# TensorE in program order through the sparse attention of a two-block model

## The chip, the cores and the metric

The kernel runs on one core of a Trainium2 chip. The metric is the device time of an execution in microseconds; each time is the median of several runs. All times inside the core count from the start of the profiled span.

## What is computed

Two blocks with two layers each work on 512 tokens of width 1024. The change is in the first block, in its sparse attention, which runs once a layer, so twice. Cut to what matters here:

```
q_rope = partial_rope(rmsnorm(heads(nq, 8)))          # 8 heads of 64, 2 key/value heads
o_cmp = softmax(q_nope @ kc.T * scale, cmp_mask) @ vc  # compressed keys
o_slc = selected_attn(q_rope, k_sl, v_sl, sel)         # top 16 of 8 blocks: all of them
o_win = window_attn(q_rope, k_wn, v_wn)                # window 512: all of the past
o_nsa = g[0] * o_cmp + g[1] * o_slc + g[2] * o_win
y_nsa = o_nsa * silu(nz)
h = h + concat([y_hg, y_nsa]) @ w_out
gate = sigmoid(rmsnorm(h) @ w_pg);  h = h + gate * (p @ w_pp)
```

With 8 blocks of 64 tokens the top 16 are all blocks, so the selected and the window branch are both causal attention over 512 tokens, with keys and values of their own.

## The kernel before

All products of a dense layer are split in a high and a low part of 32-bit floats: a dense product of 128 output columns is 24 matmuls of 512 columns (`acc_fm`, three for each of 8 tiles of the input), in two halves of 12 (`lin_steps`). The weights come in pieces of 512 KB through four buffers, and are split into `whi` (ScalarE) and `wlo` (VectorE, for `nz`, `hgo` and `hz` GpSimd) in two buffers each.

`nsa_pairs` does the two full branches. Heads are taken as four pairs `j`; a pair's two heads lie in the upper and the lower 64 partitions. For each pair the 512 queries are taken in four tiles of 128, from the last (t = 3) to the first, and a tile sees 128 (t + 1) keys. A unit is one tile with one branch (t = 3 and 2) or with both (t = 1 and 0), so a pair has six units with 512, 512, 384, 384, 2 x 256 and 2 x 128 columns for each head, and a layer has 24.

A unit has two parts. `probs` makes the scores of both heads with three products each and adds the causal mask by a product with the identity (L1317, L1319), takes the row maxima on VectorE (L1324, L1326), the exponentials with their sums on ScalarE (L1331), the reciprocal sums times the gate on VectorE (L1335 to L1339), and scales the probabilities, head 0 on VectorE (L1341), head 1 on ScalarE (L1342). `values` transposes the probabilities on TensorE (L1356), copies the transposes out of PSUM, head 0 on VectorE (L1362), head 1 on ScalarE (L1360), and multiplies with the values into one bank for the whole pair (L1369). A pair's last unit adds the compressed branch (L1372, L1373), multiplies with the gate (L1375) and splits. `values` runs two units behind `probs` (`DEEP`).

Between the units, `pump` takes a step of the generator `first_fill`: half a dense product (`nz`, `hgo`, `hz`, four blocks each, then the first part of `ple`), and behind it, as long as there are some, a small stage: the compressed attention `nsa_cmp`, its split, or `hgrn_out` (transposes, L1141). When `nsa_pairs` begins, 21 such steps are left. `APUMP` says after which unit one is taken, `pump(99)` takes the rest, and `begin` starts the first block of the output projection with 7 of its 8 tiles. Behind `nsa_pairs` follow the second part of `ple` and the rest of the projection.

The text of the program is not the order on the engines. A planner orders each engine's instructions: of those that it holds to be ready by its own clock it takes the one that stands first in the program, and `high_priority` (the weight split) goes ahead of all. An engine then runs its list strictly in that order. In `manual_schedule` the named engines keep the program's order, and the others stay the planner's.

PSUM has two banks for dense products and six (`xbank`) for all else: two for a unit's scores, two for its transposes, one for a pair's values.

Of the kernel before, what the change touches and what calls it, by code (L numbers as in the profile page):

```python
# [20 lines left out]
TT = 4  # L21
# [318 lines left out]
class Kern:  # L340
# [768 lines left out]
        self.pump()  # L1109

    DEEP = 2
    APUMP = tuple(map(int, "001111111010011101101111"))
    HPUMP = (1,) * 16

    def stat_cols(self, ps, sq, o, rhs):
# [182 lines left out]
    def nsa_pairs(self, l, begin):  # L1298

        nc = self.nc  # L1300
        mm = nc.tensor.matmul
        po = [None]

        def probs(j, t, bs):

            ts = slice(t * 128, (t + 1) * 128)
            n = 128 * (t + 1)
            nb = len(bs)
            nm, sm = self.small([128, 2, 2], "nm", bufs=4), self.small([128, 2, 2], "sm", bufs=4)
            Ss = [self.xbank("S") for _ in range(2)]  # L1310
            bb = slice(bs[0], bs[-1] + 1)
            os = [S[:, :nb * n].rearrange("p (b s) -> p b s", b=nb) for S in Ss]
            qh, ql = self.q1[j]

            for i, (x, k) in enumerate(((qh, self.kh), (ql, self.kh), (qh, self.kl))):
                for o, hs in zip(os, HALVES):
                    mm(o, lhsT=x[hs, ts], rhs=k[hs, bb, :n], start=i == 0, stop=False)  # L1317
            for o in os:
                mm(o[:, :, n - 128:], lhsT=self.identb, rhs=self.c["causal"][:, None, :].to_broadcast([128, nb, 128]),  # L1319
                   start=False, stop=True)  # L1320
            Ps = {}
            rq = self.rq[:, j, t]
            for hd in range(2):
                nc.vector.tensor_reduce(nm[:, :nb, hd], Ss[hd][:, :nb * n].rearrange("p (u s) -> p u s", u=nb),  # L1324
                                        axis=AX, op=OP.max, negate=True)
            nc.vector.tensor_tensor(nm[:, :nb], nm[:, :nb], rq[:, None, :].to_broadcast([128, nb, 2]), op=OP.mult)  # L1326
            for hd in range(2):
                P = self.slot("P")
                for i, b in enumerate(bs):
                    c = slice(i * n, i * n + n)  # L1330
                    nc.scalar.activation(P[:, c], Ss[hd][:, c], AF.Exp, scale=rq[:, hd:hd + 1], bias=nm[:, i, hd:hd + 1],  # L1331
                                         accum_out=sm[:, i, hd:hd + 1])
                    Ps[b, hd] = P[:, c]
            s = sm[:, :nb]
            nc.vector.tensor_scalar(s, s, 1e-30, 4.0, op0=OP.max, op1=OP.mult)  # L1335
            nc.vector.reciprocal(s, s)
            o = j * 6 + 2 + bs[0] * 2
            g = self.gth[:, t, o:o + nb * 2].rearrange("p (b h) -> p b h", h=2)
            nc.vector.scalar_tensor_tensor(s, g, 1.0, s, op0=OP.add, op1=OP.mult)  # L1339
            for i, b in enumerate(bs):  # L1340
                nc.vector.tensor_scalar(Ps[b, 0], Ps[b, 0], sm[:, i, 0:1], None, op0=OP.mult)  # L1341
                nc.scalar.activation(Ps[b, 1], Ps[b, 1], AF.Copy, scale=sm[:, i, 1:2])  # L1342
            return Ps

        def values(j, t, bs, Ps):
            ts = slice(t * 128, (t + 1) * 128)
            n = 128 * (t + 1)
            if t == TT - 1 and bs[0] == 0:
                po[0] = self.xbank("no")
            PTs = []  # L1350
            for hd in range(2):
                pt = self.xbank("pt")
                for k, b in enumerate(bs):
                    for i in range(t + 1):
                        s = slice(i * 128, (i + 1) * 128)
                        nc.tensor.transpose(pt[:, k * n + i * 128:k * n + (i + 1) * 128], Ps[b, hd][:, s], self.ident)  # L1356
                PT = self.slot("PT")
                m = len(bs) * n
                if hd:
                    nc.scalar.activation(PT[:, :m], pt[:, :m], AF.Copy)  # L1360
                else:
                    nc.vector.tensor_copy(PT[:, :m], pt[:, :m])  # L1362
                PTs.append(PT)
            last = t == 0
            for k, b in enumerate(bs):
                for i in range(t + 1):
                    for hd in range(2):
                        v = self.vt[i][:, b * 128 + hd * 64:b * 128 + hd * 64 + 64]
                        mm(po[0][hd * 64:hd * 64 + 64, ts], lhsT=v, rhs=PTs[hd][:, k * n + i * 128:k * n + (i + 1) * 128],  # L1369
                           start=t == TT - 1 and b == 0 and i == 0, stop=False)  # L1370
            if last:
                mm(po[0], lhsT=self.vc[0], rhs=self.pc[j], start=False, stop=False)  # L1372
                mm(po[0], lhsT=self.vc[1 + j % 2], rhs=self.pc[j], start=False, stop=True)  # L1373
                O = self.slot("on")
                nc.vector.tensor_tensor(O, po[0], self.nzg[j], op=OP.mult)  # L1375
                self.yn.append(self.split(O, "y"))

        branches = [((0, 1),), ((0, 1),), ((0,), (1,)), ((0,), (1,))]
        units = [(j, t, bs) for j in range(4) for t in reversed(range(TT)) for bs in branches[t]]
        n = len(units)  # L1380
        Ps = {}
        for i in range(n + self.DEEP):
            if i < n:
                Ps[i] = probs(*units[i])
            if i == n:
                self.pump(99)
                begin()
            if i >= self.DEEP:
                values(*units[i - self.DEEP], Ps.pop(i - self.DEEP))
            self.pump(self.APUMP[i] if i < n - 1 else 0)  # L1390


    def second(self, l):
# [491 lines left out]
```

## Time and profile before

| | us |
|---|---|
| median of 3 runs (2693.06 to 2696.95) | 2694.63 |
| profiled execution | 2693.26 |
| its span | 2691.5 |
| TensorE busy (99% of the span) | 2663.3 |
| VectorE busy (57%) | 1534.0 |
| ScalarE busy (42%) | 1142.1 |
| GpSimd busy (19%) | 499.0 |

TensorE's matmuls are pipelined and the ends of their records are modelled, so that a matmul's length overlaps the next one's: what a piece of work takes is read from its start to the start of the next. Lengths on the other engines can be read as they stand. In a row, `x8` is a group of neighbouring instructions of one kind; a bracket at its end is idle time before it and what ended that.

### The profile page before, as it was taken

Reading aid. Unit: us, or ns where it says so; the run is one execution under the profiler, and the core shown is the slowest. Engines: PE = TensorE matmul, PEld = TensorE weight load, DVE = VectorE, ACT = ScalarE, POOL = GpSimd, SP = SyncE. Lnnn points to the kernel's source line nnn. Section 1 sums busy time; section 2 is a strip of 40 time slices with the busy share of each in tenths; the row PEclk is TensorE's granted clock in tenths of the full one; section 3 lists DMA queues with packets and bytes.
Section 4 is the critical chain, followed back from the end, with each engine's and each line's share of the span. In section 5 each row is a group of like instructions: output and inputs, shape, how many; then the busy total and the mean of one; then the engine's idle time right before and its main releaser. Section 6 shows DMA issues by size and latency. Waiting matters only on the chain. (4 is left out here: it accounts for less than half of the span.)

```text
span 2691.5 us, 34626 instructions
## 1 busy us (share of the span) xinstructions
PE 2663.3 (99%) x13574; PEld 2199.9 (82%) x13574; DVE 1534.0 (57%) x2310; ACT 1142.1 (42%) x2017; POOL 499.0 (19%) x430
## 2 busy tenths in 40 slices
PE   9999999999999999999999999999999999999998
PEld 7897678888767888888888888888888888888887
DVE  6687547687754655555555444446555555544444
ACT  5656645475664533334443222233433344422223
POOL 1254221045332141110001000114111100100001
PEclk9999999999999999999999999999999999999999
DMA  4311123321112322334413333332233441333232
GB/s 170 105 43 37 39 71 102 96 87 40 32 55 86 102 86 88 108 94 126 124 57 99 97 94 97 96 105 86 87 105 99 126 126 47 102 101 95 95 95 92
DMA packets 71890, 241.79 MB, mean 90 GB/s; under 512 B 8496, under 2 KB 11824, under 8 KB 71728
## 3 DMA queue, kind: packets, MB, share of 16 engines
q1 hardware_dynamic: 70288, 234.86, 28.1%
q0 software_dynamic: 1440, 4.72, 0.5%
q8 instruction: 108, 1.77, 0.3%
q14 instruction: 54, 0.44, 0.0%
HBM read 237.45 MB, written 2.10 MB: 89 GB/s over the span
## 5 line engine op out<-in xcount | busy, mean ns | idle before, releaser
L425 ACT ACTIVATE whi<-wraw 128x1024 fp32r<-128x1024 f32 (+2 forms) x433 | 453.0, 1047 | 1103.8 <-issue 536.7
L427 DVE TENSOR_TENSOR wlo<-wraw,whi 128x1024 fp32r<-128x1024 f32 (+2 forms) x409 | 562.0, 1374 | 177.5 <-ACT whi L425 173.9
L465 PE MATMUL lin_w<-xh,wlo 128*128 128x512 f32 x704 | 273.9, 389 | 0.0
L464 PE MATMUL lin_w<-xl,whi 128*128 128x512 f32 x704 | 273.9, 389 | 0.0
L463 PE MATMUL lin_w<-xh,whi 128*128 128x512 f32 x704 | 273.9, 389 | 0.0
L1505 POOL TENSOR_TENSOR fa<-fa,fb 128x512 f32<-128x512 f32 x44 | 61.1, 1388 | 613.7 <-DVE fb L610 463.1
L463 PEld LDWEIGHTS lin_w<-xh,whi 128*128 128x128 f32 x704 | 132.2, 188 | 27.6
L464 PEld LDWEIGHTS lin_w<-xl,whi 128*128 128x128 f32 x704 | 132.2, 188 | 27.5
L465 PEld LDWEIGHTS lin_w<-xh,wlo 128*128 128x128 f32 x704 | 132.2, 188 | 27.3
L464 PE MATMUL lin_w<-fyl,whi 128*128 128x512 f32 (+1 forms) x366 | 139.9, 382 | 0.9 <-DVE fyl L511 0.9
L463 PE MATMUL lin_w<-fyh,whi 128*128 128x512 f32 (+1 forms) x366 | 139.6, 381 | 0.0
L465 PE MATMUL lin_w<-fyh,wlo 128*128 128x512 f32 (+1 forms) x366 | 139.4, 381 | 0.0
L610 DVE TENSOR_TENSOR fb<-lin_w,rs 128x512 f32<-128x512 f32 x44 | 30.4, 691 | 139.0 <-PE lin_w L465 139.0
L1331 ACT ACTIVATE P<-S,nm,qkst 128x512 f32<-128x512 f32 (+3 forms) x128 | 77.5, 611 | 53.0 <-DVE nm L1326 43.8
L568 POOL TENSOR_TENSOR nacc<-sq 128x512 f32<-128x512 f32 x11 | 16.5, 1499 | 445.6 <-ACT sq L562 445.6
L427 POOL TENSOR_TENSOR wlo<-wraw,whi 128x1024 fp32r<-128x1024 f32 x24 | 57.2, 2385 | 202.3 <-ACT whi L425 163.1
L1515 DVE TENSOR_TENSOR h<-lin_w,h 128x512 f32<-128x512 f32 x40 | 27.7, 691 | 106.8 <-PE lin_w L465 106.8
L1324 DVE TENSOR_REDUCE nm<-S 128x1 f32<-128x512 f32 (+3 forms) x96 | 55.3, 596 | 45.6 <-PE S L1319 45.6
L464 PEld LDWEIGHTS lin_w<-fyl,whi 128*128 128x128 f32 x366 | 68.8, 188 | 15.3 <-DVE fyl L511 2.2
L1464 POOL TENSOR_TENSOR ga<-ga,gb 128x512 f32<-128x512 f32 x16 | 20.6, 1290 | 322.9 <-DVE gb L1463 322.9
L463 PEld LDWEIGHTS lin_w<-fyh,whi 128*128 128x128 f32 x366 | 68.8, 188 | 13.7
L465 PEld LDWEIGHTS lin_w<-fyh,wlo 128*128 128x128 f32 x366 | 68.8, 188 | 13.0
(609 smaller groups left out, 6926.7 us busy)
## 6 DMA issues: line engine op xcount, KB each, us to landing
wraw<-in_w SPq DMA_DIRECT2D x396, 512.0 KB, 3.5
wraw<-in_w SPq DMA_DIRECT2D x34, 448.0 KB, 3.2
wraw<-in_w SPq DMA_DIRECT2D x8, 256.0 KB, 5.7
mem<-in_mem POOLq DMA_DIRECT2D x8, 256.0 KB, 3.8
out<-y SPq DMA_DIRECT2D x8, 256.0 KB, 2.2
h<-in_x SPq DMA_DIRECT2D x7, 256.0 KB, 6.0
wraw<-in_w SPq DMA_DIRECT2D x4, 420.0 KB, 3.0
pin<-in_p POOLq DMA_DIRECT2D x4, 256.0 KB, 4.1
```

The source lines that it names most:

```text
L425: self.nc.scalar.activation(h[:, c], t[:, c], AF.Copy)
L427: eng.tensor_tensor(lo[:, c], t[:, c], h[:, c].bitcast(FT), op=OP.subtract)
L463: mm(ps[:, :n], lhsT=wh[:, k, :], rhs=xh[:, :n], start=a, stop=False)
L464: mm(ps[:, :n], lhsT=wh[:, k, :], rhs=xl[:, :n], start=False, stop=False)
L465: mm(ps[:, :n], lhsT=wl[:, k, :], rhs=xh[:, :n], start=False, stop=b)
L568: eng.tensor_tensor(acc[:, :n], self.nacc[:, :n], sq[:, :n], op=OP.add)
L610: self.nc.vector.tensor_tensor(t, ps, rs, op=OP.mult)
L1324: nc.vector.tensor_reduce(nm[:, :nb, hd], Ss[hd][:, :nb * n].rearrange("p (u s) -> p u s", u=nb), axis=AX, op=OP.max, negate=True)
L1331: nc.scalar.activation(P[:, c], Ss[hd][:, c], AF.Exp, scale=rq[:, hd:hd + 1], bias=nm[:, i, hd:hd + 1], accum_out=sm[:, i, hd:hd + 1])
L1464: nc.gpsimd.tensor_tensor(gs[0], gs[0], gs[1], op=OP.add)
L1505: nc.gpsimd.tensor_tensor(a, a, b, op=OP.mult)
L1515: nc.vector.tensor_tensor(self.h[m], ps, self.h[m], op=OP.add)
```

## The change

Inside `nsa_pairs`, TensorE's instructions keep the order of the program. `values` is cut in two: `turn` (transposes and their copies) and `values` (the products). A turn of the loop is now: scores and masks of unit i, transposes of unit i - 2, one step of the fill, values of unit i - 2. `APUMP` takes a step in turns 1 to 20 and none in 0 and 21 to 23; the last step comes in turn 24 and `begin` in turn 25, between transposes and values of the last two units.

```diff
-    APUMP = tuple(map(int, "001111111010011101101111"))
+    APUMP = tuple(map(int, "011111111111111111111000"))
...
-        def values(j, t, bs, Ps):
-            ts = slice(t * 128, (t + 1) * 128)
+        def turn(t, bs, Ps):
+
             n = 128 * (t + 1)
-            if t == TT - 1 and bs[0] == 0:
-                po[0] = self.xbank("no")
             PTs = []
             for hd in range(2):
                 pt = self.xbank("pt")
...
                 PTs.append(PT)
-            last = t == 0
+            return PTs
+
+        def values(j, t, bs, PTs):
+            ts = slice(t * 128, (t + 1) * 128)
+            n = 128 * (t + 1)
+            if t == TT - 1 and bs[0] == 0:
+                po[0] = self.xbank("no")
             for k, b in enumerate(bs):
...
-            if last:
+            if t == 0:
...
-        for i in range(n + self.DEEP):
-            if i < n:
-                Ps[i] = probs(*units[i])
-            if i == n:
-                self.pump(99)
-                begin()
-            if i >= self.DEEP:
-                values(*units[i - self.DEEP], Ps.pop(i - self.DEEP))
-            self.pump(self.APUMP[i] if i < n - 1 else 0)
+
+
+        with self.tc.manual_schedule(engines={mybir.EngineType.PE}):
+            for i in range(n + self.DEEP):
+                if i < n:
+                    Ps[i] = probs(*units[i])
+                u = i - self.DEEP
+                if u >= 0:
+                    PTs = turn(*units[u][1:], Ps.pop(u))
+                if i == n:
+                    self.pump(99)
+                elif i == n + 1:
+                    begin()
+                else:
+                    self.pump(self.APUMP[i])
+                if u >= 0:
+                    values(*units[u], PTs)
```

## Rows read from the trace of the kernel before

**Rows 1.** Windows view of the stretch in either layer: busy us (instructions) by engine, clock, DMA.

```profile
211.54:380.52 168.98, 163.11 (x1033) 116.65 (x1033) 103.98 (x271) 100.39 (x235) 52.91 (x48) 0.99 0.12 39
664.76:833.80 169.04, 163.15 (x1033) 116.84 (x1033) 103.95 (x271) 100.38 (x235) 52.39 (x46) 0.99 0.15 45
```

**Rows 2.** TensorE timeline: start, length, instruction group, count; values in one piece.

```profile
232.07 1.09 PE L1369 MATMUL no<-PT,vt 128*64 128x128 f32 x16
233.10 0.50 PE L1317 MATMUL S<-kh,q1h 64*128 64x512 f32 x1
```

**Rows 3.** TensorE timeline: a unit's transposes, dense work, values in two pieces, next scores.

```profile
298.36 1.04 PE L1356 MATMUL pt<-c_ident,P 128*128 128x128 f32 x8
299.15 0.47 PE L464 MATMUL lin_hgo<-xl,whi 128*128 128x512 f32 x1
299.47 0.39 PE L465 MATMUL lin_hgo<-xh,wlo 128*128 128x512 f32 x1
...
301.08 0.39 PE L463 MATMUL lin_hgo<-xh,whi 128*128 128x512 f32 x1
301.40 0.43 PE L1369 MATMUL no<-PT,vt 128*64 128x128 f32 x2
301.76 0.49 PE L464 MATMUL lin_hgo<-xl,whi 128*128 128x512 f32 x1
302.19 1.09 PE L1369 MATMUL no<-PT,vt 128*64 128x128 f32 x14
303.21 0.51 PE L465 MATMUL lin_hgo<-xh,wlo 128*128 128x512 f32 x1
303.64 0.50 PE L1317 MATMUL S<-kh,q1h 64*128 64x512 f32 x2
...
304.77 0.82 PE L1356 MATMUL pt<-c_ident,P 128*128 128x128 f32 x6
```

**Rows 4.** TensorE timeline: one head's scores of a unit, alone, up to the next dense product.

```profile
249.15 0.50 PE L1317 MATMUL S<-kh,q1h 64*128 64x512 f32 x1
...
250.08 0.47 PE L463 MATMUL lin_hgo<-xh,whi 128*128 128x512 f32 x1
```

**Rows 5.** Waits view of TensorE over the first layer's stretch.

```profile
PE pt L1356 <- DVE sm L1335: 2.3, 1, 2.3
PE S L1317 <- ACT P L1331: 1.6, 1, 1.6
PE lin_wout L463 <- ACT yh L510: 0.8, 1, 0.8
PE no L1369 <- ACT PT L1360: 0.8, 1, 0.8
PE lin_wpp L463 <- ACT pp L865: 0.2, 1, 0.2
```

**Rows 6.** TensorE timeline: the first of the 14 units, scores and transposes.

```profile
226.98 0.44 PE L1317 MATMUL S<-kh,q1h 64*128 64x384 f32 x2
...
227.82 1.04 PE L1356 MATMUL pt<-c_ident,P 128*128 128x128 f32 x8
```

**Rows 7.** ScalarE timeline: copies of transposes behind exponentials, three units.

```profile
231.25 0.59 ACT L1360 ACTIVATE PT<-pt 128x512 f32<-128x512 f32 x1
...
299.81 0.67 ACT L1331 ACTIVATE P<-S,nm,qkst 128x384 f32<-128x384 f32 x1 [2.63 <-DVE nm L1326]
...
300.48 0.66 ACT L1331 ACTIVATE P<-S,nm,qkst 128x384 f32<-128x384 f32 x1
...
301.12 0.59 ACT L1360 ACTIVATE PT<-pt 128x512 f32<-128x512 f32 x1
...
306.98 0.56 ACT L1331 ACTIVATE P<-S,nm,qkst 128x256 f32<-128x256 f32 x1 [2.63 <-DVE nm L1326]
...
309.16 0.49 ACT L1360 ACTIVATE PT<-pt 128x384 f32<-128x384 f32 x1
```

**Rows 8.** VectorE timeline: the multiply of the maxima held up.

```profile
322.92 0.84 DVE L1326 TENSOR_TENSOR nm<-nm,qkst 128x2 f32<-128x2 f32 x1
```

**Rows 9.** GpSimd timeline at the same time.

```profile
322.45 1.29 POOL L793 TENSOR_TENSOR th<-th 128x512 f32<-128x512 f32 x1
```

**Rows 10.** Windows view around two waits of TensorE; PEclk is the granted clock's share.

```profile
217.60:221.00 3.40, 1.08 (x7) 0.69 (x7) 3.29 (x13) 3.08 (x6) 1.56 (x3) 1.00 0.00 0
344.60:348.00 3.40, 3.40 (x15) 2.08 (x17) 1.93 (x9) 3.04 (x11) 0.00 (x0) 0.54 0.00 0
348.00:351.40 3.40, 3.40 (x22) 2.46 (x21) 1.16 (x6) 1.53 (x7) 0.00 (x0) 0.95 0.03 7
```

**Rows 11.** Waits view of SyncE's queue in the stretch.

```profile
SPq L399 <- POOL wlo L427: 126.4, 8, 24.1
```

## The prediction

> **What bounds the kernel now.** I read the page first, then the windows view around the code that changes, then TensorE's timeline there, then its waits, and last the timelines of ScalarE, VectorE and GpSimd for the same units. The page says that TensorE is busy all the time; the stretch view shows where the change acts. From the first score product of the sparse attention to the last product before the output projection runs on undisturbed, a layer takes 168.98 us, and the second layer 169.04 [rows 1]. VectorE and ScalarE are busy 104 and 100 us of it, so neither has the throughput to be the bound. TensorE's busy time there, 163 us, hides how it is spent: the rows of the timeline are to be read from start to start.
>
> There, blocks of one kind are cheap when whole and dear when cut. Value products: 16 in a row take 1.03 us [rows 2], but a unit cut into 2 and 14, with dense work between, takes 0.36 + 1.02 [rows 3]; a single dense product caught between two value pieces takes 0.43 instead of 0.23. 20 of the 24 units are cut like this. Scores: the two heads sit in different row halves, and a whole unit of 512 columns with its masks takes 1.13 us for both heads [rows 3]; a head run alone takes 0.93 [rows 4], so a unit in two pieces costs 1.8. 12 or 13 units of 24 are in pieces. Real waits are few: the five listed make 5.7 us [rows 5].
>
> **What the change would leave of that.** I add up the stretch as if each block were whole, in the new order, per layer:
> - Scores with masks: 1.02 us for a first kind of unit (512 columns, narrow mask: the 1.13 less 0.11 for the narrower mask, an estimate), 0.84 for 384 columns [rows 6], 1.13, and 0.77 for 256 columns (estimated from these).
> - Transposes: 8 take 0.79 [rows 3], so 6 take 0.59 and 4 take 0.39.
> - Values: 1.03, and in proportion 0.77 and 0.52.
> - With 8, 8, 4 and 4 units: 8 x 2.84 + 8 x 2.20 + 4 x 2.95 + 4 x 1.68 = 58.8 us; the four pairs of closing products at about 0.57 (two times 0.23 and the change of kind) 2.3. Together 61.1.
> - Half a dense product is 12 instructions. Nine take 2.25 us with both ends [rows 3], three more add 0.23 each: 2.94. There are 21 halves, 61.7 us. Another 48 (21 of the first output block, 3 that close it, 24 of the second part of `ple`) at 0.23 and some ends: 11.5.
> - The compressed attention's score and transpose products and `hgrn_out`'s transposes: about 6 (24 transposes at 0.1, 27 small products, their changes of kind; an estimate).
>
> The sum is 140.3 us, so 28.7 of the 169.0 are pieces and waits. Nothing of the arithmetic goes: the gain is only the wholeness of blocks.
>
> What comes in is waiting. TensorE now stands where the program says, and what is queued behind a waiting instruction is everything. Four places:
>
> *Values behind ScalarE's copy, units 5 to 20.* Between a unit's transposes and its values lie only the 12 dense instructions. The second head's transposes are copied by ScalarE, which in every unit of the trace did so right after the exponentials of the unit just scored: scored block ends, VectorE's maxima, two or four exponentials, then the copy. From the start of the transposes to the end of that copy it took 3.35 us for one unit (298.36 to 301.71) and 4.88 for the next (304.77 to 309.65), where four exponentials stand ahead [rows 3, 7]. Over 14 units in a row, from 4.02 (227.82 to 231.84) to that 4.88, the mean is 4.50 [rows 6, 7]. The transposes' own 0.65 (mean) and the dense 2.94 cover 3.6. By the undisturbed rows, with 3.95 (two long exponentials) and 3.6 (four short ones) as estimates between them for the kinds not shown, and 0.15 to see the copy (an estimate), the six units of a head pair wait 0.4, 0.75, 0, 0, 1.5 and 0.2: 2.85, which is 7.6 for 16 units. By the mean it is 1.05 each, 17. Lower bound: 0, if ScalarE's order changes. I take 10, nearer to the undisturbed rows, because a dense product will end at the same place of every second unit, so the weight split and the evacuation that now fall between exponentials and copy fall behind the copy. Not all of it: GpSimd's operations hold VectorE's small multiply of the maxima (322.92, 0.84 us long, which ends with the GpSimd operation that began at 322.45) [rows 8, 9], and such an operation follows each product.
>
> *The last three scored units.* `APUMP` ends in 000: no dense work is between their transposes and values. The waits are 3.35, 4.88 and 3.6, plus 0.15, less the transposes: 2.7, 4.4 and 3.2, some 10. Lower bound 4 (the copy ahead of the exponentials), upper 12 (three times 4.50 and 0.15 less 0.65). The trace before waited 1.6 and 0.8 thereabouts [rows 5]. Nothing from behind the region can fill them, since `ple`'s second weights need the buffer that the 21st half frees.
>
> *The start.* Unit 0's transposes waited 2.3 [rows 5]; ahead of them now stand one dense half and compressed scores, as before. I take 2.5, from 1 to 6, since four rounds of compressed attention now sit in four neighbouring units, and their VectorE chain stands in TensorE's way.
>
> *The end.* The last output chain is as before: 0.8 + 0.8 + 0.2 [rows 5], taken as 1.8.
>
> To these I add 1.5 for TensorE's clock: after the 1.6 us wait it was granted 0.54 of full speed over 3.4 us (1.2 GHz nearly throughout), and 0.95 in the next 3.4 [rows 10], so one fall costs up to 1.6; the three waits of the tail should bring one a layer. Lower bound 0, as around the longer wait at the start the clock stayed at 1.00 [rows 10]; upper 5.
>
> The other moves cost nothing I can price. `hz`'s two input loads on GpSimd's queue and all weight loads keep their order on their queues; the issue of a weight load waits for a free buffer, 8 times 126.4 us in all behind GpSimd's split [rows 11], so the loads have slack. The first output block's products move from ahead of the last two units' transposes to behind them and cover them as before.
>
> New stretch: 140.3 + 10 + 10 + 2.5 + 1.8 + 1.5 = 166.1 us, 2.9 less per layer, 5.8 in all. From the profiled execution's 2693.26 (span 2691.5) that gives 2687.5; the median of the runs, 2694.63, is 1.4 above that execution, so about 2689.
>
> **Rivals.**
> - *ScalarE copies before it exponentiates.* The waits of steady units fall to 1, the tail's to 4, the clock to 0.5: 140.3 + 1 + 4 + 2.5 + 1.8 + 0.5 = 150, 19 less per layer: 2657. For it: the transposes end at 299.15 and the exponentials begin at 299.81 [rows 3, 7], so a copy could go first. Against: no unit of the trace has that order.
> - *Slower: the values wait as long as the mean of before says.* Place: the value products. 17 in steady units, 12 in the tail, 5 of clock, 4 at the start, 1.8: 180, 11 more per layer: 2717. It decides from a mean wait of 0.8 us per steady unit on, since 28.7 less the other 15.8 leaves 12.9 for 16 units; that is a copy that ends 4.25 us after the transposes begin. For it: the mean is 4.50. Against: part of that mean is work which the new order moves.
> - *The clock swings all through the region.* A wait in each steady unit, and each with a fall like the one seen, 1.6 x 16 = 26 more per layer than forecast: 2741. Against: after the 2.3 us wait there was none. Beside this stands a rule of the Trainium skill ("TensorE: Matmul & The Clock Gate", section "A second HAM failure mode: psum-queue depth-cycling"): short idle times between groups of matmuls, often repeated as PSUM buffers are cycled, make the clock go back and forth between its two levels. By that rule it would be this rival's time; the trace shows one fall in the stretch and so bears it out only in part.
> - *TensorE's stream stays much as it is*, because six shared PSUM banks already force it: 2694.
>
> **How the numbers follow.** Forecast 0.42 (its own range 2674 to 2704), faster rival 0.24, slower 0.24, clock 0.04, unchanged 0.06. 0.2% is 5.4 us, about what a measurement of this kernel can tell from no change. The forecast splits into 0.20 faster, 0.15 within, 0.07 slower. Faster: 0.20 + 0.24 = 0.44; same: 0.15 + 0.06 = 0.21; slower: 0.07 + 0.24 + 0.04 = 0.35. Range 2658 to 2717: it leaves out the clock rival and half of each of the two others' far sides.
>
> **What would show it.** After: every score block of six in a row, every unit's values in one piece of at most 1.05 us; a wait of 0 to 1.5 us ahead of the values, released by ScalarE's copy, longest in units with four exponentials; 3 to 4 us in units 21 to 23; the granted clock below 1 there and nowhere else. Wrong would be: values that never wait in steady units (faster rival), transposes or scores that wait instead (the probabilities or the banks are late), or a clock below 1 between the tails.

## The result: slower, by 0.65%

The changed kernel takes 2713.38 us (median of 4 runs, 2712.15 to 2714.62) against 2695.79 before (4 runs): the ratio is 1.0065, with an interval from 1.0052 to 1.0079. The forecast was 2689. The time lies close to the slower rival's 2717, and the profile shows that rival's place: the products with the values wait for copies. The profiled execution took 2713.28 (span 2711.2, 19.7 more than before).

Nearly all of it arises in the two stretches. The windows view of the changed kernel [rows 1]; columns: length, then busy time (instructions) of TensorE, its weight load, VectorE, ScalarE and GpSimd, then granted clock and DMA:

```profile
212.05:391.08 179.03, 157.46 (x1033) 118.66 (x1032) 106.72 (x271) 100.98 (x235) 52.74 (x48) 0.92 0.12 37
675.36:853.52 178.16, 156.71 (x1033) 118.04 (x1033) 106.56 (x271) 101.08 (x235) 52.52 (x46) 0.93 0.14 42
```

They are 10.0 and 9.1 us longer, with TensorE busy about 6 us less (blocks are whole) and at a lower clock. The waits view of TensorE over the first stretch (sum, count, longest) [rows 5]:

```profile
PE no L1373 <- ACT PT L1358: 13.4, 11, 1.9
PE no L1373 <- DVE PT L1360: 4.8, 3, 2.5
PE ptc L1258 <- DVE Pc L1287: 1.5, 1, 1.5
PE pt L1354 <- DVE P L1341: 1.4, 1, 1.4
PE lin_wpp L463 <- ACT pp L865: 0.2, 1, 0.2
```

The value products (L1373; "values" below) now wait 14 times for the copies of the transposes, mostly for ScalarE's (L1358); before there was one such wait of 0.8. Below, "turn i" is the round of the loop that scores unit i and transposes unit i - 2, and "the dense half" is its step of the fill, 12 products. TensorE's timeline in turn 13, from the transposes on [rows 3]:

```profile
295.38 0.61 PE L1354 MATMUL pt<-c_ident,P 128*128 128x128 f32 x4
295.74 0.49 PE L463 MATMUL lin_hz<-xh,whi 128*128 128x512 f32 x1
...
298.38 0.39 PE L465 MATMUL lin_hz<-xh,wlo 128*128 128x512 f32 x1
298.70 0.43 PE L1373 MATMUL no<-PT,vt 128*64 128x128 f32 x2
300.62 0.65 PE L1373 MATMUL no<-PT,vt 128*64 128x128 f32 x6 [1.49 <-ACT PT L1358]
301.20 0.50 PE L1376 MATMUL no<-pcs,vch 128*128 128x512 f32 x1
```

and ScalarE's in the same turn [rows 7]:

```profile
297.11 0.78 ACT L1331 ACTIVATE P<-S,nm,qkst 128x512 f32<-128x512 f32 x1 [2.90 <-DVE nm L1326]
...
297.87 0.77 ACT L1331 ACTIVATE P<-S,nm,qkst 128x512 f32<-128x512 f32 x1
...
298.63 1.06 ACT L425 ACTIVATE whi<-wraw 128x1024 fp32r<-128x1024 f32 x1
299.60 0.70 ACT L1342 ACTIVATE P<-P,sm 128x512 f32<-128x512 f32 x1
300.21 0.36 ACT L1358 ACTIVATE PT<-pt 128x256 f32<-128x256 f32 x1
```

The dense half is over at 298.70. The copy starts at 300.21, though its transposes were over by 295.74: ahead of it stand two exponentials, a weight split and the scaling of the probabilities. TensorE does nothing else meanwhile, because the next instruction in the program is the rest of the values.

The three turns without dense work, in TensorE's timeline:

```profile
358.10 0.82 PE L1354 MATMUL pt<-c_ident,P 128*128 128x128 f32 x6
360.21 0.43 PE L1373 MATMUL no<-PT,vt 128*64 128x128 f32 x2 [1.29 <-DVE PT L1360]
362.52 1.54 PE L1373 MATMUL no<-PT,vt 128*64 128x128 f32 x10 [1.88 <-ACT PT L1358]
...
365.34 1.49 PE L1354 MATMUL pt<-c_ident,P 128*128 128x128 f32 x6
...
368.66 1.54 PE L1373 MATMUL no<-PT,vt 128*64 128x128 f32 x10 [1.13 <-ACT PT L1358]
370.13 1.97 PE L1354 MATMUL pt<-c_ident,P 128*128 128x128 f32 x8
371.75 0.78 PE L463 MATMUL lin_wpp<-ph,whi 128*128 128x512 f32 x1
```

In turn 22 the waits make 3.2 us; behind them six transposes have a length of 1.49, where they had 0.82. The clock column of the windows view (the last but two) says why [rows 10]:

```profile
320.20:327.00 6.80, 4.68 (x27) 3.66 (x27) 2.69 (x10) 3.73 (x12) 0.38 (x1) 0.50 0.00 0
361.13:374.78 13.65, 11.11 (x51) 8.78 (x52) 4.19 (x15) 5.87 (x20) 0.00 (x0) 0.50 0.00 0
374.80:378.20 3.40, 3.40 (x29) 2.59 (x28) 1.14 (x1) 2.41 (x5) 0.00 (x0) 1.00 0.00 0
```

From 361.13 on, in the waits of turn 22 and behind them, TensorE was granted 1.2 GHz (0.50) for 13.65 us, in and behind the waits of turn 16 for 6.8, and for 6.8 more near the start: 27.3 us in this layer and 23.9 in the other, where before it was 3.4 in each.

### The profile page after: what moved, and what is told of

It reads as the page before. It is cut to its first block, busy times and chain, and to the rows that moved or that the text cites. A ratio compares the mean times of both kernels' runs of the same rounds, so it can differ in the third digit from the quotient of the medians.

```text
span 2711.2 us, 34626 instructions
## 1 busy us (share of the span) xinstructions
PE 2651.2 (98%) x13574; PEld 2202.8 (81%) x13574; DVE 1538.4 (57%) x2310; ACT 1143.1 (42%) x2017; POOL 500.0 (18%) x430
## 4 chain that ended last, share of the span: by engine, by line
PE 92%; DVE 3%; ACT 3%; issue 1%; POOL 0%; DMA 0%; SPq 0%; ACTq 0%; DVEq 0%; POOLq 0%
PE lin_w L464 9%; PE lin_w L463 9%; PE lin_w L465 9%; PE no L1373 2%; ACT P L1331 1%; PE lin_xq L464 1%; PE lin_xq L463 1%; PE lin_wpg L464 1%; PE lin_wo L464 1%; PE lin_ga L463 1%; PE lin_gb L463 1%; PE lin_gc L463 1%; PE lin_wy L463 1%; PE lin_wpg L465 1%; PE lin_ga L464 1%; PE lin_ga L465 1%
## 5 line engine op out<-in xcount | busy, mean ns | idle before, releaser
L427 DVE TENSOR_TENSOR wlo<-wraw,whi 128x1024 fp32r<-128x1024 f32 (+2 forms) x409 | 562.9, 1377 | 166.3 <-ACT whi L425 162.6
L1373 PE MATMUL no<-PT,vt 128*64 128x128 f32 x640 | 61.3, 298 | 36.3 <-ACT PT L1358 26.6
L1373 PEld LDWEIGHTS no<-PT,vt 128*64 128x64 f32 x640 | 42.3, 145 | 56.8 <-ACT PT L1358 33.1
```

What stands on the lines that cost most here:

```text
L427: eng.tensor_tensor(lo[:, c], t[:, c], h[:, c].bitcast(FT), op=OP.subtract)
```

## The experiments

Theory: in program order the values wait for ScalarE's copy, and the idle time brings the clock down. Rivals: the distribution of the dense pieces (none in the last turns), the new loop itself, or VectorE's and GpSimd's part in making the probabilities. "Stretch" is the length from the first score product to the end of `ple`, in the first and the second layer, from TensorE's timeline (before 169.1 and 169.2, changed 179.2 and 178.3). Each ratio is to the kernel before, run on the same chip. The kernel before took 2694.8 to 2696.9 us on the chips used, so between two rows a difference of some 2 us says nothing by itself. "Later" stands for values one turn later, "empty turns" for those without a dense half.

| kernel | us | ratio (95%) | stretch |
|---|---|---|---|
| order left to the planner | 2691.08 | 0.9981 (0.9972 to 0.9990) | 167.4, 168.4 |
| old loop in order | 2894.02 | 1.0731 (1.0715 to 1.0747) | 270.0, 268.9 |
| values a turn later | 2673.61 | 0.9915 (0.9900 to 0.9930) | 159.2, 159.3 |
| copies first | 2706.78 | 1.0036 (1.0026 to 1.0046) | 176.6, 174.6 |
| copies on VectorE | 2681.11 | 0.9947 (0.9933 to 0.9962) | 163.5, 162.1 |
| idle work in the last waits | 2706.90 | 1.0046 (1.0031 to 1.0061) | 176.5, 176.6 |
| later, empty turns spread | 2683.43 | 0.9955 (0.9938 to 0.9971) | 163.5, 164.7 |
| the same, copies on VectorE | 2685.19 | 0.9962 (0.9947 to 0.9977) | 166.1, 166.3 |
| maxima first | 2722.22 | 1.0096 (1.0081 to 1.0111) | 182.7, 183.7 |
| later, maxima first | 2671.65 | 0.9908 (0.9892 to 0.9925) | 156.9, 158.3 |
| the same, empty turns at 5, 9, 13 | 2682.67 | 0.9949 (0.9935 to 0.9964) | 162.6, 163.1 |
| idle work at the start | 2714.31 | 1.0067 (1.0052 to 1.0082) | 178.5, 180.0 |
| compressed chain first | 2713.97 | 1.0063 (1.0048 to 1.0078) | 179.6, 178.4 |
| maxima first from unit 4 | 2709.92 | 1.0049 (1.0032 to 1.0065) | 178.7, 173.6 |
| later, maxima first from unit 4 | 2669.74 | 0.9899 (0.9885 to 0.9914) | 156.7, 156.4 |
| the same, compressed chain first | 2664.92 | 0.9882 (0.9867 to 0.9896) | 153.8, 155.0 |
| splits on VectorE | 2709.10 | 1.0048 (1.0031 to 1.0065) | 177.6, 177.0 |
| later, both first, splits on VectorE | 2656.89 | 0.9856 (0.9841 to 0.9871) | 150.8, 150.5 |

**Order left to the planner.**

```diff
-        with self.tc.manual_schedule(engines={mybir.EngineType.PE}):
+        with ExitStack():
             for i in range(n + self.DEEP):
```

> The changed kernel with its new loop, its new split into transposes and values and its new distribution of dense pieces, but with TensorE's order left to the planner. Theory (the loss comes from the fixed order: values stand behind ScalarE's copy, and the idle stretches bring the clock down): the planner fills those waits with other work, and the time goes back to that of the kernel before, about 2694 us (2686 to 2702), with granted-clock records at the lower level only near the end of each attention stretch as before (some 3 to 7 us per layer). Rival A (the loss comes from the new distribution of the dense pieces, none in the last turns): about 2713 us as with the change. Rival B (what was lost lies in the new loop): about 2713 us too, and then the waits of the values in the profile stay near 29 us per layer.

2691.08: the loop and the new distribution are no loss, even a small gain. The fixed order alone costs the 22 us between this kernel and the changed one. The planner's waits view has almost none for copies:

```profile
PE ptc L1258 <- DVE Pc L1287: 2.4, 2, 1.5
PE S L1317 <- ACT P L1331: 2.2, 1, 2.2
PE no L1373 <- ACT PT L1358: 0.9, 3, 0.5
```

One detail was missed: the low clock (10.2 us a layer, expected 3 to 7) does not stand near the end. In the first layer it falls twice within the first 40 us, in the second twice there and once 113 us in.

**The old loop in program order.**

```diff
+        with self.tc.manual_schedule(engines={mybir.EngineType.PE}):
             for i in range(n + self.DEEP):
...
```

> The kernel before with its own loop and its own distribution of dense pieces, but TensorE in program order for the whole loop: a unit's values follow directly behind its own transposes, with no dense half between. Theory: each unit's values wait the whole way from the transposes' start to the copy's end (3.4 to 6 us, of which about 0.8 is covered by the second head's transposes), some 2.5 to 4 us over 24 units, 60 to 95 us per layer less the 28.7 us of split pieces, and the clock falls in most of the stretch: 2760 to 2850 us. Rival (program order in itself costs little, the new placing of the pieces is what costs): 2700 us or less.

2894.02, beyond the theory's upper end. Without a dense half between, nearly every unit waits for both copies:

```profile
PE no L1369 <- DVE PT L1362: 37.8, 21, 5.9
PE no L1369 <- ACT PT L1360: 23.0, 20, 1.9
```

What was underrated is the clock, at the lower level for 112.6 of the 270.0 us, in 19 separate falls inside the first stretch. The Trainium skill, "TensorE: Matmul & The Clock Gate", section "A second HAM failure mode: psum-queue depth-cycling", describes this: short idle times between groups of matmuls, repeated often, make the clock go to and fro between its two levels. This trace agrees with it. The changed kernel, with three and four falls, lies between this one and the kernel before, with one.

**Values one turn later.**

```diff
-                    PTs = turn(*units[u][1:], Ps.pop(u))
+                    PTs[u] = turn(*units[u][1:], Ps.pop(u))
...
-                if u >= 0:
-                    values(*units[u], PTs)
+                if u >= 1:
+                    values(*units[u - 1], PTs.pop(u - 1))
```

> The changed kernel with the values of each unit one turn later than its transposes (the loop is one turn longer), TensorE still in program order. Theory: the copies end 3.4 to 8.4 us after their transposes begin, a whole turn lasts over 5 us, so nearly all of the 30 us per layer of waits ahead of values go, and with them the low clock of the steady part; left are the start, the end and the last turns without a dense piece: 145 to 158 us per layer against 178, in all 2645 to 2680 us. Rival (the dense distribution or the chain of the other engines sets the pace): the waits move to the scores or the transposes, 2700 to 2715 us.

2673.61: 40 us faster than the change and 22 faster than before. In turns 4 to 20 the values and the dense half ahead of them are longer than when whole and undisturbed (1.02, 0.81 or 0.59, and 2.94) by 17.0 us in the changed kernel and by 0.6 here. What is left waits for other things:

```profile
PE S L1317 <- ACT P L1331: 4.5, 3, 2.2
PE ptc L1258 <- DVE Pc L1287: 2.6, 2, 1.5
PE pt L1354 <- DVE P L1341: 1.1, 1, 1.1
```

The stretch stayed 1 us over the expected 158.

**The copies ahead of the exponentials.**

```diff
+                with self.tc.high_priority(offset=300):
                     if hd:
                         nc.scalar.activation(PT[:, :m], pt[:, :m], AF.Copy)
...
```

> The changed kernel with both copies of the transposes given to the planner ahead of the exponentials of the same turn on their engines. Theory: head 1's copy on ScalarE then ends about 2.0 to 2.7 us after the transposes begin rather than 3.4 to 6, inside the dense half that covers some 3.6, so the 19 us of values' waits in the steady part fall to 0 to 4 per layer, the last units keep 2 to 5, the exponentials come 0.7 us later and stand off the path: 2675 to 2690 us. Rival (exponentials are on the path, the probabilities then come late for the next transposes): the waits move to the transposes, 2705 to 2720 us.

2706.78 (nine runs, from 2701.5 to 2710.4): the theory's number failed, and so did the rival's mechanism, since it is still values that wait (10.8 us for ScalarE's copies and 4.8 for VectorE's). ScalarE's timeline in turn 13 shows how far a priority goes:

```profile
297.09 1.05 ACT L425 ACTIVATE whi<-wraw 128x1024 fp32r<-128x1024 f32 x1
298.04 0.38 ACT L1359 ACTIVATE PT<-pt 128x256 f32<-128x256 f32 x1
298.30 0.72 ACT L1342 ACTIVATE P<-P,sm 128x512 f32<-128x512 f32 x1
```

The copy passed the scaling, but not the weight split and, in turns with two exponentials, not these (of four it passed one). The wait of turn 13 fell from 1.9 to 1.3, but those of turns 8 and 14 rose from 0 and 0.4 to 1.5. It was no clean test of the theory; the next is.

**Both copies on VectorE.**

```diff
-                    nc.scalar.activation(PT[:, :m], pt[:, :m], AF.Copy)
+                    nc.vector.tensor_copy(PT[:, :m], pt[:, :m])
```

> The changed kernel with both copies of the transposes on VectorE, where no exponential stands ahead of them. Theory: head 1's copy then ends about 0.65 us behind head 0's, that is 2.0 to 3.4 us after the transposes begin where ScalarE's took 3.3 to 6.0; the dense half and the transposes cover 3.6 of it, so the steady waits (19 us per layer) fall to 2 to 6, those of the three turns without dense work (8.7) to about 5, and with them half of the low-clock time: 2668 to 2688 us. Rival (it is VectorE with its maxima and splits that holds the units, not ScalarE's copy): the waits stay under another name, 2700 to 2716 us.

2681.11, as the theory said: 32 of the 40 us that values a turn later gives, though VectorE is busier by 11 us a layer. The lengthening in turns 4 to 20 is 7.3 us. So it was the place in ScalarE's queue, behind the exponentials, and not the copying.

**The clock after the last waits.**

```diff
+                if 20 < i < n:
+                    clk = self.xbank("clk")
+                    for k in range((9, 14, 9)[i - 21]):
+                        mm(clk.rearrange("p (b s) -> p b s", b=4), lhsT=self.identb,
+                           rhs=self.c["causal"][:, None, :].to_broadcast([128, 4, 128]), start=True, stop=True)
```

> The changed kernel with idle work put into its last three waits only: 9, 14 and 9 products of 512 columns (the mask product's operands, into a bank that nobody reads) between the dense piece's place and the values in the three turns without dense work, about 2.0, 3.1 and 2.0 us, a little less than the waits there. It prices the clock alone. Theory: the clock stays up there, the 13.7 and 10.2 us at the lower level after these waits go, and the work in them (transposes 1.49 and 1.97 for 0.57 and 0.80, values 1.54 and 1.13 for 0.69, the first products of the ple output 3.1 for 1.6) comes back to its own length: 3 to 4 us per layer, 2704 to 2709 us, although more is executed. Rival (the waits absorb what the low clock costs): 2712 to 2718 us.

2706.90, inside the theory's range: 32 more products a layer, and 6.5 us less (5 by the ratios). The windows from the scores of turn 22 to the end of `ple`, first the changed kernel, then this one (columns as in the first windows):

```profile
356.98:391.24 34.26, 29.53 (x152) 22.10 (x152) 12.33 (x27) 14.28 (x35) 0.20 (x1) 0.80 0.05 17
```

```profile
359.69:389.92 30.23, 29.34 (x175) 20.41 (x175) 12.32 (x27) 14.30 (x35) 0.20 (x1) 1.00 0.06 19
```

VectorE and ScalarE do the same work; the clock of 0.80 costs 4.0 us here, and 2.6 in the second layer (38.1 to 35.5 from the scores of turn 21 on). The profiled execution, 2709.92, is the longest of the four: in its first layer the clock fell in turn 7 as well, where in the changed kernel it fell only in the second layer. That fall costs some 1.5 us (turns 4 to 15 take 77.2 us with it, 75.6 without).

**The clock at the start.**

```diff
+            if t == 0 and hasattr(self, "nsa_warm"):
+                self.nsa_warm(pt, 6)
...
+                if first and hd == 0:
+                    warm(pt, 6)
```

> The changed kernel with idle work in the two waits at the start of the stretch: six products of 512 columns (1.35 us) ahead of the compressed attention's first transposes and six ahead of unit 0's, written into the bank that the transposes then fill. It prices the clock at the start: after the waits of 1.5 and 1.4 us it is at the lower level for 6.8 us (3.4 in the second layer), the transposes take 1.72 for 0.80 and the dense half 4.6 for 2.9. Theory: that goes, 1.5 to 2.7 us per layer: 2707 to 2711 us. Rival (the compressed attention's chain on VectorE holds the next block anyway): 2712 to 2717 us.

2714.31: the rival. At the start the clock is at the lower level nowhere any more, and the first four turns take 25.3 us in both layers (25.8 and 24.8 in the changed kernel). What the clock gives back there is waited for again: the start hangs on the chain of the other engines.

**VectorE's order.** First the maxima ahead of everything, in the changed kernel and with values a turn later.

```diff
+            with self.tc.high_priority(offset=300):
                 for hd in range(2):
                     nc.vector.tensor_reduce(nm[:, :nb, hd], Ss[hd][:, :nb * n].rearrange("p (u s) -> p u s", u=nb),
                                             axis=AX, op=OP.max, negate=True)
...
```

> The changed kernel with the maxima of the scores given to the planner ahead of VectorE's other work. In turn 16 two splits of a dense input (1.91 and 1.17 us) run between and ahead of the maxima, the exponentials start about 4 us late, TensorE idles 4.1 us and its clock is at the lower level for 6.8 us. Theory (VectorE's order is a second cause beside ScalarE's copy): the exponentials of that turn start 1.2 to 3 us earlier, the wait shrinks by as much: 2 to 4 us less in each layer, 2705 to 2710 us. Rival (the planner starts the splits before the scores are ready, so priority changes nothing): 2712 to 2715 us.

> The kernel with values a turn later, with the maxima ahead of VectorE's other work as well. Theory: its wait of the scores behind the same splits (2.5 us and 3.4 us of low clock per layer) goes in part: 2666 to 2671 us. Rival: no change, 2672 to 2675 us.

2722.22: slower, which neither side expected. The maxima of units 0 and 1 passed the compressed attention's chain:

```profile
PE ptc L1258 <- DVE Pc L1287: 3.9, 1, 3.9
PE ptc L1258 <- ACT Pc L1279: 2.7, 1, 2.7
```

The first four turns take 30.5 and 30.9 us. The order is only part of the first wait, which was 1.5. The chain's last multiply on VectorE starts 0.9 us later than in the changed kernel, counted from the start of the stretch, and lasts 2.58 us instead of 1.14 (0.42 in the next rounds). It now lies beside GpSimd's weight split:

```profile
218.91 2.58 DVE L1287 TENSOR_TENSOR Pc<-Pc,csm 128x256 f32<-128x256 f32 x1
218.86 2.35 POOL L427 TENSOR_TENSOR wlo<-wraw,whi 128x1024 fp32r<-128x1024 f32 x1
```

In turn 16 the maxima did end 1.2 us earlier. With values a turn later the ratio's interval overlaps that of the kernel without priority, so the time alone decides nothing; the trace has 11.1 us for turns 16 and 17 (14.9 without) and 28.9 for the first four (24.5).

Then the same from unit 4 on, with either place of the values:

```diff
+            with self.tc.high_priority(offset=300) if j or t < 2 else ExitStack():
```

> The changed kernel with the maxima of the scores first on VectorE, but only from unit 4 on. With all units it lost 8.8 us against the change: the first four turns took 30.5 and 30.9 us for 25.8 and 24.8, the rest was 0 to 0.6 us shorter per layer. Theory: the loss lay in the start alone, and what is left is the small gain of turns 4 to 17: 2711 to 2714 us, that is, VectorE's order matters little while ScalarE's copy holds the values. Rival (the maxima's priority costs in the steady part too): 2716 to 2722 us.

> The kernel with values a turn later, with the maxima first from unit 4 on. With all units its first four turns took 28.9 and 30.3 us for 24.5 and 24.7, turns 4 to 17 took 79.5 for 86.0. Theory (once ScalarE's copy no longer holds the values, the maxima behind VectorE's splits are the next bound): both gains stay, 5 to 6 us less per layer than with values later alone: 2660 to 2665 us. Rival (the gain of turns 4 to 17 came from the longer start, which let VectorE and ScalarE catch up): 2669 to 2675 us.

2709.92, 1 us below the expected range: the loss was the start alone (25.0 and 25.6 us again). 2669.74 misses the theory: turns 16 and 17 keep their gain (11.1), but turns 4 to 15 take 72.4 us, where they took 68.4 behind the longer start. The rival was right on that part.

**The compressed attention's chain ahead**, in the changed kernel and on top of the last.

```diff
+        with self.tc.high_priority(offset=300):
             nc.vector.tensor_tensor(f(P), f(S), self.rq[:, :4, t, :, None].to_broadcast([128, 4, 2, 32]), op=OP.mult)
...
```

> The changed kernel with the compressed attention's chain on VectorE and ScalarE (product with the query scale to the normalized probabilities) ahead of their other work. Theory (the start's waits of 1.5 and 1.4 us come from VectorE, where the maxima of units 0 and 1 stand in the middle of that chain): the chain ends 1.5 to 2.5 us earlier, the first wait goes, unit 0's probabilities come later by part of it; 1 to 3 us less per layer: 2707 to 2711 us. Rival (VectorE's operations are stretched there by GpSimd's four of 4.0 us in all, so that order changes nothing): 2712 to 2716 us.

> The same with the compressed attention's chain first as well. Theory: 1 to 3 us less per layer at the start: 2654 to 2662 us. Rival (that chain delays unit 0's and unit 1's probabilities by as much): within 2 us of the same kernel without it.

2713.97: nothing, since VectorE's order at the start came out as it was. 2664.92 is 4.8 us less than without it, a gain of which the first four turns have none on average (23.9 and 25.0 us for 24.6 and 24.4); turns 4 to 15 have it (70.3 for 72.4), so the theory's place was wrong.

**GpSimd.** Part of the start is explained by two rows of the changed kernel, VectorE's

```profile
219.45 2.31 DVE L1339 SCALAR_TENSOR_TENSOR sm<-gth,sm 128x2 f32<-128x2 f32 x1
```

and GpSimd's

```profile
219.32 2.42 POOL L427 TENSOR_TENSOR wlo<-wraw,whi 128x1024 fp32r<-128x1024 f32 x1
```

An operation of 0.16 us lasts 2.31 and ends at 221.76, GpSimd's split at 221.74. The Trainium skill, "SBUF — State Buffer", section "SBUF: two separate sides", names an exclusive lock: of a VectorE operation with two SBUF inputs and a GpSimd operation that reads SBUF, the one that starts first holds it for its whole length, and the other waits. The rows agree, GpSimd's being the first by 0.13 us. The chain of work that ended last in the changed kernel has this place and turn 16 in it (start, length):

```profile
219.53 2.24 DVE sm L1339
...
314.98 1.91 DVE pl L511
```

```diff
-                eng = self.nc.gpsimd if key[0] in ("nz","hgo","hz") else self.nc.vector
+                eng = self.nc.vector
```

> The changed kernel with the weight splits of the attention's dense work (nz, hgo, hz) on VectorE instead of GpSimd: 1.38 us each there for 2.4. Theory (GpSimd holds VectorE: at the start a small operation of 0.16 us lasts 2.31 and ends together with the GpSimd split that began at 219.32, in turn 16 a split of 0.7 to 1.2 lasts 1.91 the same way): these stretched operations go, unit 0's probabilities come about 1 us earlier and the exponentials of turn 16 about 0.7, at the price of 1.4 us on VectorE per half, which has room: 1 to 3 us less per layer, 2706 to 2711 us. Rival (VectorE pays as much as it gains, its splits now stand in front of maxima): 2712 to 2720 us.

> The kernel with values a turn later, the maxima first from unit 4 on and the compressed attention's chain first, with the same splits on VectorE. Theory: the start's waits (2.4 and 1.7 us per layer there) shrink, 1 to 2 us less per layer: 2660 to 2664 us. Rival: VectorE's added 1.4 us per half stand in the chain of probabilities: 2666 to 2675 us.

2709.10, as expected: the first four turns fall to 23.5 and 23.4 us, and the same operation takes 0.16 us:

```profile
219.25 0.16 DVE L1339 SCALAR_TENSOR_TENSOR sm<-gth,sm 128x2 f32<-128x2 f32 x1
```

Turn 16 hardly gained: the multiply of its maxima ends 4.85 us after the masks, where it was 5.42. Without GpSimd's splits the fastest version falls by 8 us to 2656.89, more than either side expected. It is 1.4% below the kernel before, and its stretch needs

```profile
212.08:363.00 150.92, 145.17 (x1034) 110.44 (x1034) 108.82 (x279) 99.83 (x236) 33.84 (x40) 0.99 0.14 43
```

**Spreading the turns without dense work** failed three times: with values a turn later, then with the copies on VectorE too, then with the maxima first and empty turns at 5, 9 and 13.

```diff
-    APUMP = tuple(map(int, "011111111111111111111000"))
+    APUMP = tuple(map(int, "011111011111011111011111"))
```

> The kernel with values a turn later, and its three turns without dense work spread: turns 6, 12 and 18 instead of 21 to 23. Theory: an isolated turn without dense work waits little, because its chain of exponentials has two full turns around it, and the tail's waits of scores and its slow transposes (some 4.5 us per layer) go: 2662 to 2670 us. Rival (each such turn waits as a tail turn does, wherever it stands, since ScalarE needs about 3 us per unit): 2671 to 2680 us.

> The kernel with values a turn later and the empty turns spread, and both copies on VectorE as well. Theory: the waits of the scores for the exponentials (4.5 us per layer with values a turn later, since ScalarE frees their banks late) shrink by the 0.6 us per unit that ScalarE no longer spends: 2655 to 2668 us. Rival (the maxima on VectorE now come later by as much and hold the exponentials): no gain over the same kernel with ScalarE's copy, or a loss of 2 to 8 us against it.

> The same with the turns without dense work at 5, 9 and 13 rather than at 21 to 23, so that none falls together with the splits of turns 16 to 19 (when they stood at 6, 12 and 18, turns 6 and 12 lost 0.9 us each and turn 18 lost 6 us beside its own clock). Theory: the three cost 0.9 us each instead of some 4.5 at the end: 2 to 3 us less per layer than with them at the end, 2660 to 2668 us. Rival (an empty turn pushes a later split or evacuation into the chain of probabilities again): 2672 to 2685 us.

2683.43, 2685.19 and 2682.67; the first and the last differ only by this from kernels with the empty turns at the end, which take 2673.61 and 2671.65. Turns 6 and 12 lost 0.9 us each, as an isolated turn should; but turn 18 met VectorE's two splits of `pin`, and the next scores waited 4.9 us for the exponentials that free their banks. With empty turns at 5, 9 and 13 it was the split of a closed head pair (1.43 us between maxima and multiply, the scores of turn 10 took 3.9). The copies on VectorE gained nothing on top (the four runs lie at 2682 and at 2688): the rival.

## Why the prediction was wrong

The sum per layer, by its own terms, for the first layer. Measured is what a block takes from its start to the start of the next in TensorE's timeline, less its length when whole and undisturbed. The last row but one is what is left of the stretch.

| term | forecast | slower rival | measured |
|---|---|---|---|
| whole blocks | 140.3 | 140.3 | taken as 140.3, see below |
| values behind the copy, turns 4 to 20 | 10 | 17 | 17.0 |
| turns 21 to 23, transposes and values | 10 | 12 | 10.5 |
| start | 2.5 | 4 | 6.0 |
| low clock beside these | 1.5 | 5 | 3.9 |
| end, and what remains | 1.8 | 1.8 | 1.3 |
| stretch | 166.1 | 180 | 179.0 |

*Right:* the price of whole blocks. Undisturbed scores take 1.02, 0.84, 1.12 and 0.78 us, eight transposes 0.80, the dense half 2.84 to 2.94, values 1.02, 0.81 and 0.59 (forecast 1.03, 0.77, 0.52); with most waits gone the fastest version has a stretch of 150.8. Right too were the three turns at the end, the place of the waits, and that nothing waits for loads.

*The step that failed* is "I take 10, nearer to the undisturbed rows", with its reason that the weight split and the evacuation "fall behind the copy". The term measured 17.0, and these 7.0 us are the largest part of the 12.9 by which the stretch exceeds the forecast (start 3.5, clock 2.4, last turns 0.5, and 0.5 less at the end). The undisturbed rows held for most kinds of turn: with four long exponentials 1.4 and 1.2 us in turns 4 and 10 (forecast 1.5), with 384 columns or in the last unit of a pair 0 to 0.6 (forecast 0 to 0.2). But in turns 7, 13 and 19 the split and the scaling stood ahead of the copy: 2.3, 1.9 and 1.9, forecast 0.75. And turn 16 cost 5.5, forecast 1.5; there VectorE splits the `pin` input around its maxima, and its own copy comes last:

```profile
314.98 1.91 DVE L511 TENSOR_TENSOR pl<-pin,ph 128x512 fp32r<-128x512 f32 x1
317.42 1.17 DVE L511 TENSOR_TENSOR pl<-pin,ph 128x512 fp32r<-128x512 f32 x1
319.78 0.41 DVE L1326 TENSOR_TENSOR nm<-nm,qkst 128x4 f32<-128x4 f32 x1
320.11 0.55 DVE L1360 COPY PT<-pt 128x384 f32<-128x384 f32 x1
```

These four turns took 11.7 us, where the rows gave 3.75. Turn 18 took 1.5 for 0.4: an evacuation and an output split went ahead of its exponentials. Turn 4 makes it 17 turns, where the forecast counted 16.

That the copy comes "in every unit" right after the exponentials was a misreading of the trace before, as ScalarE's timeline in turn 8 there shows:

```profile
263.65 0.66 ACT L1331 ACTIVATE P<-S,nm,qkst 128x384 f32<-128x384 f32 x1
...
264.30 1.05 ACT L425 ACTIVATE whi<-wraw 128x1024 fp32r<-128x1024 f32 x1
265.25 0.61 ACT L1342 ACTIVATE P<-P,sm 128x384 f32<-128x384 f32 x1
265.75 0.59 ACT L1360 ACTIVATE PT<-pt 128x512 f32<-128x512 f32 x1
```

From the transposes' start to the copy's end this unit took 6.45 us, and in turn 13, where split and scaling stand ahead of the copy too, 5.65. So the mean that the rival used contained just such work, and the change did not move it out of the way. Added up again, that mean is 4.41 and not 4.50, which gives 15.4 us rather than 17; that the rival's 17 was met to the decimal is partly luck, since it stands for 16 equal waits and eight of the 17 turns hardly wait. The mean wait came to 1.0 us per turn, above the 0.8 from which the rival decided.

*The start* was 6.0 for 2.5: two waits (1.5 and 1.4) and longer blocks around them. That it is not the clock was shown (filled up, no change); that GpSimd's split is part of it was shown (1.4 to 2.3 us less without it); that the place of the maxima on VectorE matters was shown only in the bad direction, and there 1.4 us of the first wait arise beside GpSimd's split again. The rest, some 3.6 us, is put down to the compressed attention's chain; that is argued from the waits view and not separated.

*The clock* was taken too small: 3.9 us for 1.5, of which 1.1 lies in turn 17 and 2.8 from turn 23 on, and part of the other rows is clock too. The 1.5 stood for one fall among the last turns of each layer; it was 13.65 and 10.2 us at the lower level, worth 4.0 and 2.6 us. The falls at the start, in turn 16 and, in the second layer, in turn 7 (some 1.5 us) were not foreseen; the one at the start cost nothing.

Of the rivals, "ScalarE copies before it exponentiates" did not occur and could not be forced by the priority tried. The clock did swing, in four places and not in each unit.

What stays open: that rest of the start, why turns 4 to 15 are shorter behind a longer start, and whether the maxima put first would lose anything at the start without GpSimd's splits, which no run tried.

## What to carry to other kernels

An order written by hand must put as much other work between a producer and its consumer as the queue of the engine between them is long; here one turn's lag more turned a loss of 0.65% into a gain of 0.85%, with nothing else changed. When a wait is estimated from a mean and from a few clean rows, list what makes the others longer, and drop it only where the new order shows a place for it. A low clock cost time here only where the slowed blocks were the path; idle work put into the wait tells the two cases apart.

## What was not expected of the hardware

- A VectorE operation on 128 x 2 elements lasted 2.31 us instead of 0.16 beside a GpSimd operation of 2.42, and its own 0.16 once that was gone.
- TensorE did 32 products more in the last waits, and the same stretch from turn 22 on was 4.0 us shorter in the first layer: its clock stayed at 1.00 rather than 0.80.
- At the start the granted clock went from 0.50 to 1.00 with no effect on the time (25.3 us for 25.8 and 24.8).
